# Scan loads by direction, two and three half steps ahead, and weights, sums and gates loaded through GpSimd's queue, in a one-core conformer, state-space and expert block

## The chip, the cores and the metric

The kernel runs on one core of one Trainium2 chip. The metric is the device time of one execution in microseconds; lower is better. The kernel before took 3031.84 us (median of three runs, 3028.96 to 3038.07).

## What is computed

A block of 1040 tokens (16 of them prepended) by 1024 features goes through an input projection of 9280 columns, which feeds a convolution branch (31 taps) and a two-way state-space scan in chunks of 128 tokens; both are gated, merged, added, and then a mixture of 16 experts follows. Cut to what matters here:

```python
proj = einsum('btd,dk->btk', rms_norm(h), w_in)           # conv, z, xbc, dt, gates
c = conf_a * sigmoid(conf_g); c = depthwise_conv(c, w_conf_dw, b_conf_dw)
xbc = silu(depthwise_conv(xbc, w_ssm_conv, b_ssm_conv))   # 7 taps -> xs, B, C
# per direction, chunk of 128 and group of 8 heads (32 heads, 4 groups):
decay  = exp(where(mask, a_cs[l] - a_cs[s], -inf))
y_diag = einsum(C, B, decay, xd);  state = state * exp(a_cs[-1]) + B^T (decay_to_end * xd)
y_off  = einsum(C, state_before, exp(a_cs))
y = rms_norm((y_forward + y_backward + d_skip * xs) * silu(z))
h = h + (gate0 * (silu(layer_norm(c)) @ w_conf_out) + gate1 * (y @ w_ssm_out)) @ w_out
out = rms_norm(h + expert_choice_ffn(rms_norm(h)))
```

## The kernel before

The program is one function, `tile_block`. Its stages follow one another: the input is normalized and transposed (to some 45 us); the 73 column tiles of the input projection run, and from about 137 us on the state-space scan runs between them (to 1227 us); then the two output projections and the merge (to some 1750 us); then the experts. The change touches the second stage alone.

**The projection.** `Columns` holds the order of the 73 weight tiles (128 columns each, 1024 by 128 values of 4 bytes). `group` loads three tiles at a time (L194), squares them on ScalarE (L196), sums the squares over partitions with a small matmul (L202) and makes scales (L206 to L212). `convert` splits a tile in a high and a low half-precision part, the first on ScalarE (L223), the second on VectorE (L224). `take` is called once per tile: at every third tile it calls `group` for the next three, and it converts one tile ahead. Six buffers hold loaded tiles (`wraw` and `wraw2`, three each). A tile is then multiplied in three chunks of some 346 tokens, 24 matmuls of 128x346 each (`proj`, L97 to L99), into three PSUM buffers named `mm`.

**What a tile is for.** `do_conf` takes two tiles for one block of the convolution, writes the gated input `ci` (L326), and puts 30 taps (L334, one VectorE instruction over 1040 tokens each) and the store of the result into the list `taps`; `some_taps(n)` takes n from it. `ci` has one buffer, and `do_conf` begins by emptying the list. `xbc_tile` writes `pre` (L374), makes six taps (L380), a silu (L381) and stores; its transposes (`turn`, L395 and L399) come eight thirds of a tile later. `z_tile` and `gate_tile` write `st` (L345, L355 to L357) and store it; the pool `stage` has four buffers.

**The scan.** For each of 4 groups and 9 chunks there is one unit of work within the chunk (`within`, `add_within`) and two half steps of the running state, one forward and one backward (`state`, `pass_state`): 36 units, 72 half steps. `within` loads B and C (`bc_`, L578), for both directions the running sums of the decay, repeated on all partitions (`row`, 512 KB each, L581), and the inputs `xk` (L538); ScalarE turns each `row` to decays (L599 eight times, L600), VectorE multiplies (L545, L602), and 32 matmuls of a unit add into `py` (L614). A half step loads `xk`, `Cc` (L629) and `er` (L633), multiplies the state (L646) and updates it (L652, L658, L660). `sum_of` loads the skip term `xa` (L555, ten buffers); `add_to` adds each part, and with the last one loads silu(z) into a buffer of `er` (L567), multiplies (L568) and stores `yz_d` (L569).

**What sets the order.** All loads of this stage are issued by SyncE's queue (SP), all stores by GpSimd's (POOL); a queue works in order, and an instruction that waits for a buffer holds what stands behind it. `plan` says which projection tiles lie beside each group of the scan. `fill` moves the projection on between half steps. Each instruction's place on its engine comes from a planner, which takes what is ready by its order in the program; `tc.high_priority(offset=n)` moves an instruction up by n places in that order.

The loop over half steps reads, with `prepare` as the three parts of `within`:

```python
for n, (g, d, c) in enumerate(halves):
    m = n % per
    if n % 2 == 0 and n // 2 + 1 < len(units):
        terms.append(prepare(units[n // 2 + 1]))
    with ahead():
        if n + 2 < len(halves):
            ops.append(state(*halves[n + 2]))
    if n % 2 == 0:
        add_within(*units[n // 2], terms.pop(0))
    fill(g, (m + 0.5) / per)
    S[d] = pass_state(g, d, c, S[d], ops.pop(0))
    fill(g, (m + 1) / per)
```

Of the kernel before, what the change touches and what calls it, by code (L numbers as in the profile page):

```python
# [18 lines left out]
P = 128  # L19
# [3 lines left out]
KD = 8  # L23
# [22 lines left out]
def tile_block(ctx, tc, x, meta_tokens, w_norm_mix, w_in, w_conf_dw, b_conf_dw, conf_ln_g, conf_ln_b,  # L46
# [117 lines left out]
    with tpool("upool", side="right") as upool, tpool("stage", bufs=4, side="right") as stage, \  # L164
# [11 lines left out]
        class Columns:  # L176
# [7 lines left out]
            def group(self, behind=None):  # L184
                b = self.G * self.groups
                cols = self.order[b:b + self.G]
                self.groups += 1
                n = len(cols)
# [3 lines left out]
                for i, col in enumerate(cols):  # L192
                    t = (wraw if (b + i) % 6 < 3 else wraw2).tile([P, KD, P], F32, name="wr")
                    nc.sync.dma_start(t, w_in[0][:, col:col + P].rearrange("(k p) c -> p k c", p=P))  # L194
                    with tc.high_priority(offset=400):
                        act.activation(out=junk, in_=t, func=AF.Square, accum_out=sq[:, i:i + 1])  # L196
                    self.raw[b + i] = t
                sqb = wsm.tile([P, 4], BF, name="sqb")
                dve.tensor_copy(sqb[:, :n], sq[:, :n])
# [27 lines left out]
            def take(self, col):  # L227
# [4 lines left out]
                if n == 0:  # L232
                    self.group(turned)
                    self.convert(0)
                if n % self.G == 0:
                    self.group(None if n else turned)
# [75 lines left out]
        def do_conf(j):  # L312
            wa, wg = wtile(j * P), wtile(D + j * P)
            some_taps(TK)
            ci = cfp.tile([P, T + 30], F32, name="ci")
            pool.memset(ci[:, 0:15], 0.0)
            pool.memset(ci[:, T + 15:T + 30], 0.0)
            for t0, n in NCH:
# [8 lines left out]
                yield  # L327
            co = cfp.tile([P, T], F32, name="co")
# [162 lines left out]
        def c_(j):  # L491
# [6 lines left out]
                z_(14, 15) + c_(5) + g_(9, 10) + c_(6) + g_(11, 12) + c_(7) + g_(13, 14, 15)]  # L498
# [18 lines left out]
        with tpool("b1") as b1:  # L517
# [12 lines left out]
            with tpool("s2", bufs=2) as s2, tpool("sps", bufs=1, space=PSUM) as sps:  # L530
# [4 lines left out]
                def load_xk(g, c):  # L535
                    L = TOK[c][1]
                    xk = s2.tile([P, 640], F32, name="xk", bufs=3)
                    nc.sync.dma_start(xk[:L], xk_d[g][c, :L])  # L538
                    return xk

                def scaled(g, xk, c, w, d):
# [3 lines left out]
                    dve.tensor_mul(heads(o[:L]), heads(xk[:L, :512]),  # L545
# [13 lines left out]
                def add_to(g, c, y):  # L559
                    t0, L = TOK[c]  # L560
                    s = sums[g, c]
                    dve.tensor_add(s[0][:, :, :L], s[0][:, :, :L], y[:, :, :L])
# [824 lines left out]
```

## Time and profile before

| | |
|---|---|
| runs, us | 3028.96, 3031.84, 3038.07 |
| profiled execution, us | 3033.02, span 3031.3 |
| mean granted TensorE clock | 0.956 of full speed |
| TensorE matmul (PE) busy | 2757.7 us, 91% |
| VectorE (DVE) busy | 2245.9 us, 74% |
| ScalarE (ACT) busy | 1714.3 us, 57% |
| GpSimd (POOL) busy | 501.3 us, 17% |

The profile is of one execution. A view by stretches gives the busy time of each engine in a part of the span; a table of waits tells which engine stood idle, before which line, and what released it; a timeline shows single instructions with the idle time ahead of them. L97 is line 97 of the kernel before.

### The profile page before, as it was taken

The page shows a single profiled execution, that of the slowest core. Times are in us where ns is not written, and L with a number is a line of the kernel's source. Part 1 is how long each engine was busy: PE and PEld are TensorE (multiplying, and loading weights), DVE is VectorE, ACT ScalarE, POOL GpSimd, SP SyncE. Part 2 cuts the span into 40 slices and gives each one's busy share as a digit, 9 for nine tenths or more (in the row PEclk, how much of TensorE's full clock was granted, in tenths as well). Part 3 has the DMA queues.
Part 4 walks back from the last instruction along what each step waited for, and adds up shares of the span by engine and source line. Part 5 has one row for each costly group of instructions (what it writes and reads, how often), then busy time and mean ns, then how long its engine had stood idle before and what let it go on. Part 6 is the DMA issues. An engine that isn't in the chain of part 4 may idle for free. (4 is left out here: it accounts for less than half of the span.)

```text
span 3031.3 us, 65413 instructions
## 1 busy us (share of the span) xinstructions
PE 2757.7 (91%) x27584; PEld 2364.2 (78%) x27584; DVE 2245.9 (74%) x3023; ACT 1714.3 (57%) x2551; POOL 501.3 (17%) x546
## 2 busy tenths in 40 slices
PE   6989989978988977889999789999999999999995
PEld 4656656655655655788978789999999999999995
DVE  6958886988996898797555678677777677777763
ACT  6657656556665531444213466666666666666643
POOL 1120021011012001341000002122221122222213
PEclk9999989989999988999999899999999999999997
DMA  5356667556658552522533889999999999999994
GB/s 145 105 157 197 182 179 212 159 163 202 190 160 242 173 163 77 174 75 74 164 116 115 294 298 335 330 333 328 329 333 333 327 337 332 331 335 335 334 322 139
DMA packets 424374, 691.89 MB, mean 228 GB/s; under 512 B 41313, under 2 KB 197825, under 8 KB 424073
## 3 DMA queue, kind: packets, MB, share of 16 engines
q1 hardware_dynamic: 386832, 584.61, 57.8%
q0 software_dynamic: 27168, 71.70, 8.1%
q10 hardware_dynamic: 10080, 31.40, 3.3%
q8 instruction: 216, 3.54, 0.5%
q14 instruction: 78, 0.64, 0.1%
HBM read 612.61 MB, written 75.01 MB: 227 GB/s over the span
## 5 line engine op out<-in xcount | busy, mean ns | idle before, releaser
L97 PE MATMUL gu<-xT,wh 128*128 128x130 f16 x3968 | 697.0, 222 | 2.3 <-ACT sil L1160 1.8
L99 PE MATMUL gu<-xT,wl 128*128 128x130 f16 x3968 | 696.0, 220 | 1.1 <-DVE wl L1131 1.1
L98 PE MATMUL gu<-xT,wh 128*128 128x130 f16 x3968 | 696.8, 219 | 0.0
L1117 ACT ACTIVATE junk<-wst 128x2048 bf16<-128x2048 f32 x248 | 473.8, 1910 | 382.6 <-DMA wst<-in_w_exp_gate_dram 317.5
L1131 DVE SCALAR_TENSOR_TENSOR wl<-wst,sc,wh 128x2048 f16<-128x2048 f32 x248 | 572.4, 2345 | 21.0 <-ACT wh L1128 17.6
L98 PEld LDWEIGHTS <-wh 128*128 128x128 f16 x4856 | 480.9, 99 | 91.7 <-issue 45.9
L97 PEld LDWEIGHTS <-wh 128*128 128x128 f16 x4856 | 475.6, 98 | 57.6 <-issue 12.5
L99 PEld LDWEIGHTS <-wl 128*128 128x128 f16 x4832 | 469.3, 97 | 45.6 <-DVE wl L1131 1.5
L1183 PE MATMUL dn<-ac,wst 128*128 128x130 f32 x3840 | 459.3, 277 | 0.0
L1183 PEld LDWEIGHTS dn<-ac,wst 128*128 128x128 f32 x3840 | 440.7, 191 | 0.0
L1202 POOL DMA_INDIRECT h<-yo,idx x60 | 186.6, 3110 | 901.9 <-DVE yo L1201 746.1
L334 DVE SCALAR_TENSOR_TENSOR co<-ci,ct,co 128x1040 f32<-128x1040 f32 x240 | 314.9, 1312 | 2.8 <-ACT co L331 0.3
L97 PE MATMUL mm<-uh,wh 128*128 128x346 f16 (+3 forms) x888 | 283.4, 319 | 31.5 <-DVE ci L326 17.3
L97 PE MATMUL mm<-uh,wl 128*128 128x346 f16 (+1 forms) x864 | 271.6, 314 | 18.2 <-ACT pre L374 9.6
L98 PE MATMUL mm<-ul,wh 128*128 128x346 f16 (+3 forms) x888 | 283.1, 319 | 0.0
L99 PE MATMUL mm<-uh,wh 128*128 128x346 f16 (+3 forms) x888 | 282.0, 318 | 0.0
L98 PE MATMUL mm<-ul,wl 128*128 128x346 f16 (+1 forms) x864 | 271.2, 314 | 0.0
L99 PE MATMUL mm<-uh,wl 128*128 128x346 f16 (+1 forms) x864 | 270.9, 314 | 0.0
L1128 ACT ACTIVATE wh<-wst,sc 128x2048 f16<-128x2048 f32 x124 | 241.3, 1996 | 17.3 <-DVE sc L1094 16.6
L599 ACT ACTIVATE row<-row,cst 128x128 f32<-128x128 f32 (+1 forms) x576 | 169.7, 378 | 116.9 <-DMA row<-cs_d 112.7
L380 DVE SCALAR_TENSOR_TENSOR po<-pre,sp,po 128x1040 f32<-128x1040 f32 x144 | 185.5, 1293 | 6.0 <-ACT po L377 5.7
L97 PE MATMUL mm<-yh,wh 128*128 128x346 f32 (+1 forms) x480 | 158.9, 338 | 25.1 <-DVE acc L802 14.9
(428 smaller groups left out, 4722.3 us busy)
## 6 DMA issues: line engine op xcount, KB each, us to landing
wst<-in_w_exp_gate_dram SPq DMA_DIRECT2D x128, 1024.0 KB, 8.2
wst<-in_w_exp_up_dram SPq DMA_DIRECT2D x128, 1024.0 KB, 8.0
wst<-in_w_exp_down_dram SPq DMA_DIRECT2D x128, 1024.0 KB, 9.8
wr<-in_w_in_dram SPq DMA_DIRECT2D x73, 512.0 KB, 4.7
row<-cs_d SPq DMA_DIRECT2D x64, 512.0 KB, 5.6
xk<-xk_d SPq DMA_DIRECT2D x92, 320.0 KB, 3.5
er<-ecs_d SPq DMA_DIRECT2D x120, 128.0 KB, 3.4
xk_d<-xt POOLq DMA_DIRECT2D x40, 256.0 KB, 3.3
```

What stands on the lines that cost most here:

```text
L97: pe.matmul(ps, wh(k), xh(k), start=(k == 0), stop=False)
L98: pe.matmul(ps, wh(k), xl(k), start=False, stop=False)
L99: pe.matmul(ps, wl(k), xh(k), start=False, stop=(k == K - 1))
L334: dve.scalar_tensor_tensor(co, ci[:, m:m + T], ct[:, m:m + 1], co, op0=OP.mult, op1=OP.add)
L380: dve.scalar_tensor_tensor(po, pre[:, m:m + T], sp[:, j, m:m + 1], po, op0=OP.mult, op1=OP.add)
L599: act.activation(out=E[:L, j, :L], in_=E[:L, j, :L], func=AF.Relu, scale=-1.0, bias=cs)
L1117: act.activation(out=junk, in_=t[m][b], func=AF.Square, accum_out=sq[:, b, m:m + 1])
L1128: act.activation(out=wh[m][0], in_=t[m][0], func=AF.Copy, scale=sc[:, 1, m:m + 1])
L1131: dve.scalar_tensor_tensor(wl[m][b], t[m][b], sc[:, 1, m:m + 1], wh[m][b], op0=OP.mult, op1=OP.subtract)
L1183: pe.matmul(last["dn"][b // 3][:, b % 3], t[:, k, b * P:b * P + P], ac[:, 2 * i + k], start=(i + k == 0 and b % 3 == 0), stop=(i == 7 and ...
L1202: nc.gpsimd.indirect_dma_start(out=h2_d[b], in_=yo[:, h], in_offset=None, compute_op=OP.add, out_offset=bass.IndirectOffsetOnAxis(ap=r.idx ...
```

## The change

Five edits, all in the projection and scan stage:

- `group` is split in `load` and `scale`. `load` still comes at every third tile; `scale` (squares, sums, scales) comes one tile later and its squares lose their high priority. All weight loads but the first three go through GpSimd's queue.
- `within` works on one direction at a time, so that there are 72 steps in place of 36 units, each beside one half step of the state. `row` and `Bk` come three, and the other scan loads two half steps ahead of their use (in the loop: the first part of a step's generators at n + 3, the second at n + 2, the computation at n + 1). The B part of `xk` (columns 512 to 639) becomes a load of its own, `Bk`; `xk` has four buffers of 512 columns instead of three of 640.
- `xa` (now nine buffers) and silu(z), now `sz` with one buffer, are loaded through GpSimd's queue. The product with silu(z) and the store of `yz_d` are put off by two thirds of a tile, and the product is written over `xa`; `er` serves the half steps alone.
- `ci` has two buffers, and `do_conf` empties the list of taps after the projection instead of before it.
- In the last group one gate tile moves from before to behind the second and third block of the convolution, six taps in place of five are taken per half step, and what is left of the transposes is done one half step earlier.

Cut to its core:

```diff
-            def group(self, behind=None):
+            def load(self):
                 b = self.G * self.groups
...
+                    (nc.gpsimd if b else nc.sync).dma_start(t, w_in[0][:, col:col + P].rearrange("(k p) c -> p k c", p=P))
+                    self.raw[b + i] = t
+
+            def scale(self, b, behind=None):
...
-                    with tc.high_priority(offset=400):
-                        act.activation(out=junk, in_=t, func=AF.Square, accum_out=sq[:, i:i + 1])
+                for i in range(n):
+                    act.activation(out=junk, in_=self.raw[b + i], func=AF.Square, accum_out=sq[:, i:i + 1])
...
                 if n % self.G == 0:
-                    self.group(None if n else turned)
+                    self.load()
+                if n % self.G == 1:
+                    self.scale(n - 1 + self.G)
...
-            some_taps(TK)
-            ci = cfp.tile([P, T + 30], F32, name="ci")
+            ci = cfp.tile([P, T + 30], F32, name="ci", bufs=2)
...
+            some_taps(TK)
             co = cfp.tile([P, T], F32, name="co")
...
-                z_(14, 15) + c_(5) + g_(9, 10) + c_(6) + g_(11, 12) + c_(7) + g_(13, 14, 15)]
+                z_(14, 15) + c_(5) + g_(9) + c_(6) + g_(10, 11) + c_(7) + g_(12, 13, 14, 15)]
...
-                        xa = s2.tile([P, 4, P], F32, name="xa", bufs=10)
-                        nc.sync.dma_start(xa[:, :, :L], xs_d[g][:, :, t0:t0 + L].rearrange("i p t -> p i t"))
+                        xa = s2.tile([P, 4, P], F32, name="xa", bufs=9)
+                        nc.gpsimd.dma_start(xa[:, :, :L], xs_d[g][:, :, t0:t0 + L].rearrange("i p t -> p i t"))
...
-                        sz = s2.tile([P, 4, P], F32, name="er")
-                        nc.sync.dma_start(sz[:, :, :L], sz_d[g][:, :, t0:t0 + L].rearrange("i p t -> p i t"))
...
+                        sz = s2.tile([P, 4, P], F32, name="sz", bufs=1)
+                        nc.gpsimd.dma_start(sz[:, :, :L], sz_d[g][:, :, t0:t0 + L].rearrange("i p t -> p i t"))
+                        finish.append((third[0] + 2, lambda: gated_out(g, c, xa, sz[:, :, :L])))
...
+                steps = [(within(*u), state(*h)) for u, h in zip(units, halves)]
...
+                for n in range(-3, len(steps)):
+                    with tc.high_priority(offset=600):
+                        for k in (3, 2):
+                            for s_ in steps[n + k] if 0 <= n + k < len(steps) else ():
+                                next(s_)
+                    if 0 <= n + 1 < len(steps):
+                        terms = [next(s_) for s_ in steps[n + 1]]
...
+                    (g, c, d), (xw, E) = units[n], ready[0]
                     m = n % per
...
+                    add_within(g, c, d, xw, E)
                     fill(g, (m + 0.5) / per)
...
+                    S[d] = pass_state(g, d, c, S[d], ready[1])
+                    ready = terms
                     fill(g, (m + 1) / per)
-                    if m == per - 3:
+                    if m == per - 4:
...
-                    some_taps((2, 4, 3, 5)[g])
+                    some_taps((2, 4, 3, 6)[g])
```

How this moves instructions shows at three places. In the rows below a name after L is the line of the kernel that the rows are of, so lines of the changed kernel are some ten to thirty higher. **SyncE's queue, between the first and the second group of the scan.** Before:

```order
L567 DMA er<-sz_d_67 128x4x128
L629 DMA Cc<-bc_d_61 128x16
L578 DMA bc__4894<-bc_d_62 128x2x128
L194 DMA wr<-in_w_in_dram 128x8x128 x2
L633 DMA er<-ecs_d 64x512 x2
L194 DMA wr<-in_w_in_dram 128x8x128
L567 DMA er<-sz_d_67 128x4x128
L581 DMA row<-cs_d 128x1024 x2
L629 DMA Cc<-bc_d_62 128x128
```

With the change (`Bk` is the B part of `xk`):

```order
L644 DMA Cc<-bc_d_61 128x16
L648 DMA er<-ecs_d 64x512 x2
L640 DMA Bk<-xk_d_76 128x128
L595 DMA bc__4650<-bc_d_62 128x2x128
L591 DMA row<-cs_d 128x8x16
L644 DMA Cc<-bc_d_62 128x128
L640 DMA Bk<-xk_d_76 128x128
L644 DMA Cc<-bc_d_62 128x128
L595 DMA bc__4924<-bc_d_62 128x2x128
L648 DMA er<-ecs_d 64x512 x2
```

The weight loads `wr` and the loads of silu(z) (`er<-sz_d`) are gone from this queue, and the `row` of one direction comes by itself, ahead of loads for later steps.

**GpSimd's queue, at the z tiles 14 and 15 in the last group.** Before there are stores alone:

```order
L358 DMA sz_d_70<-st 128x348
L358 DMA sz_d_70<-st 128x346
L569 DMA yz_d_73<-er 128x4x128
L358 DMA sz_d_70<-st 128x346
L569 DMA yz_d_73<-er 128x4x16
L358 DMA sz_d_70<-st 128x348
L358 DMA sz_d_70<-st 128x346 x2
L358 DMA sz_d_70<-st 128x348
L358 DMA sz_d_70<-st 128x346 x2
```

With the change weight loads and a load of silu(z) stand between the stores:

```order
L363 DMA sz_d_70<-st 128x348
L363 DMA sz_d_70<-st 128x346 x2
L189 DMA wr<-in_w_in_dram 128x8x128 x2
L363 DMA sz_d_70<-st 128x348
L363 DMA sz_d_70<-st 128x346 x2
L189 DMA wr<-in_w_in_dram 128x8x128
L363 DMA sz_d_70<-st 128x348
L363 DMA sz_d_70<-st 128x346
L573 DMA sz<-sz_d_70 128x4x128
L363 DMA sz_d_70<-st 128x346
L189 DMA wr<-in_w_in_dram 128x8x128 x3
```

Behind the trains of two, one and three weight loads stand the stores of `st`, which before stood behind one another.

**VectorE, at the last block of the convolution** (`co` is a tap, `ci` its input; `er`, `xa`, `S`, `xw` belong to the scan). Before:

```order
L334 SCALAR_TENSOR_TENSOR co<-ci,ct,co 128x1040 x2
L568 TENSOR_TENSOR er<-er,xa 128x512 x2
L334 SCALAR_TENSOR_TENSOR co<-ci,ct,co 128x1040 x3
L568 TENSOR_TENSOR er<-er,xa 128x4x16
L326 SCALAR_TENSOR_TENSOR ci<-sg,mm 128x348
L326 SCALAR_TENSOR_TENSOR ci<-sg,mm 128x346 x2
L224 SCALAR_TENSOR_TENSOR wh<-wr,sc,wh 128x8x128
L334 SCALAR_TENSOR_TENSOR co<-ci,ct,co 128x1040 x7
```

With the change (here the last of the three writes of `ci` alone):

```order
L614 TENSOR_TENSOR row<-row,cbm_11553 128x1024
L339 SCALAR_TENSOR_TENSOR co<-ci,ct,co 128x1040
L580 TENSOR_TENSOR xa<-xa,sz 128x512
L330 SCALAR_TENSOR_TENSOR ci<-sg,mm 128x346
L226 SCALAR_TENSOR_TENSOR wl<-wr,sc,wl 128x8x128
L339 SCALAR_TENSOR_TENSOR co<-ci,ct,co 128x1040
L667 TENSOR_TENSOR er<-yo,er 128x512
L679 TENSOR_TENSOR S_11657<-st,S_11657 128x512
L550 TENSOR_TENSOR xw<-xk,dtw 128x512
L339 SCALAR_TENSOR_TENSOR co<-ci,ct,co 128x1040
L568 TENSOR_TENSOR xa<-xa,er 128x512
```

Before, all taps of the block ahead (`co`) precede the writes of `ci`, and 30 taps are left behind the last write; with the change the write stands among them, with 54 taps behind it. Behind the first `yl` (VectorE's part of the output projection that comes next) there were 5 taps and are 27.

## Rows read from the trace of the kernel before

**Rows 1.** Engines by stretch: us, each engine's busy time (x instructions), clock, DMA, GB/s.

```profile
137.00:300.00 163.00, 146.95 (x1033) 97.85 (x1032) 113.44 (x155) 110.68 (x213) 23.25 (x51) 0.96 0.58 175
300.00:560.00 260.00, 237.43 (x1719) 161.55 (x1718) 210.83 (x300) 161.11 (x325) 32.65 (x63) 0.95 0.65 190
560.00:830.00 270.00, 234.52 (x1648) 158.17 (x1646) 242.64 (x327) 162.01 (x317) 31.37 (x66) 0.92 0.61 180
830.00:1060.00 230.00, 208.64 (x1514) 142.51 (x1514) 182.68 (x263) 141.87 (x285) 32.78 (x59) 0.95 0.66 191
1060.00:1227.00 167.00, 126.74 (x852) 85.39 (x849) 150.88 (x180) 40.90 (x85) 17.35 (x31) 0.89 0.40 120
1227.00:1300.00 73.00, 65.17 (x370) 62.99 (x368) 53.49 (x38) 40.05 (x59) 28.69 (x11) 0.91 0.52 170
```

**Rows 2.** Waits of TensorE, 137 to 1227 us: total us, times, longest.

```profile
PE mm L395 <- ACT po L381: 26.1, 6, 7.5
PE mm L97 <- DVE ci L326: 17.3, 2, 16.4
PE mm L97 <- ACT xt L399: 15.9, 7, 6.1
PE cb L587 <- DVE cbm L592: 14.3, 5, 5.8
PE mm L97 <- ACT pre L374: 11.1, 5, 5.9
...
PE mm L395 <- ACT st L356: 8.5, 2, 5.1
```

**Rows 3.** Waits of ScalarE, the same stretch.

```profile
ACT row L599 <- DMA row<-cs_d: 112.7, 32, 10.2
ACT junk L196 <- DMA wr<-in_w_in_dram: 90.1, 32, 7.2
...
ACT pre L374 <- DMA xs_d<-pre: 21.6, 6, 9.2
```

**Rows 4.** Timeline of SyncE's queue at one such place: start us, us.

```profile
428.81 0.37 SPq L567 DMA_DIRECT2D er<-sz_d  x1
429.28 0.99 SPq L581 DMA_DIRECT2D row<-cs_d  x2
```

**Rows 5.** Timeline of ScalarE, then; idle time ahead in brackets.

```profile
433.57 1.28 ACT L599 ACTIVATE row<-row,cst 128x128 f32<-128x128 f32 x4 [5.04 <-DMA row<-cs_d]
434.76 1.05 ACT L381 ACTIVATE po<-po 128x1040 f32<-128x1040 f32 x1
```

**Rows 6.** Timeline of TensorE, then, and two matmuls of a projection without waits.

```profile
239.74 0.31 PE L99 MATMUL mm<-uh,wh 128*128 128x346 f16 x1
239.88 0.31 PE L97 MATMUL mm<-uh,wh 128*128 128x346 f16 x1
...
435.87 1.02 PE L395 MATMUL mm<-ident,po 128*16 128x128 f32 x4 [5.45 <-ACT po L381]
```

**Rows 7.** Waits of SyncE's queue, 137 to 1227 us.

```profile
SPq L633 <- DMA yz_d<-er: 73.1, 15, 13.1
...
SPq L581 <- PE py L614: 42.1, 20, 6.9
```

**Rows 8.** Waits of VectorE, 137 to 1227 us.

```profile
DVE er L568 <- DMA er<-sz_d: 27.7, 19, 4.6
```

**Rows 9.** Timeline of TensorE at its longest wait.

```profile
1183.36 0.45 PE L97 MATMUL mm<-uh,wh 128*128 128x346 f16 x1 [16.39 <-DVE ci L326]
```

**Rows 10.** Groups of instructions, VectorE: count | busy us, mean ns | idle before.

```profile
L334 DVE SCALAR_TENSOR_TENSOR co<-ci,ct,co 128x1040 f32<-128x1040 f32 x240 | 314.9, 1312 | 2.8 <-ACT co L331 0.3
```

**Rows 11.** DMA issues by line: count, KB each, median us from issue to landing.

```profile
wr<-in_w_in_dram SPq DMA_DIRECT2D x73, 512.0 KB, 4.7
sz_d<-st POOLq DMA_DIRECT2D x32, 173.0 KB, 4.4
```

**Rows 12.** Timeline of GpSimd: one store as its queue issues it.

```profile
424.42 0.76 POOL L569 DMA_DIRECT2D yz_d<-er  x1
```

More of the change, by code (lines that the diff above doesn't have):

```diff
@@ L232, in take @@
                 if n == 0:
-                    self.group(turned)
+                    self.load()
+                    self.scale(0, turned)
                     self.convert(0)
                 if n % self.G == 0:
-                    self.group(None if n else turned)
+                    self.load()
+                if n % self.G == 1:
+                    self.scale(n - 1 + self.G)
                 self.convert(n + 1)
@@ new lines, in tile_block, with within @@
+                shared = {}
+                def within(g, c, d):
+                    t0, L = TOK[c]
+                    h0 = HG * g + 32 * d
+                    assert all((g, i) in turned_ for i in range(5))
+                    E = s2.tile([P, HG, P], F32, name="row", bufs=4)
+                    nc.sync.dma_start(E[:, :, :L], cs_d[c, h0:h0 + HG, :L].partition_broadcast(P))
+                    yield
+                    if d == 0:
+                        bc_ = s2.tile([P, 2, P], F32, name="bc_")
+                        nc.sync.dma_start(bc_[:, :, :L], bc_d[g][:, :, t0:t0 + L])
+                        shared[g, c] = load_xk(g, c), []
+                        sum_of(g, c)
+                    xk, cbm = shared[g, c]
+                    yield
+                    if d == 0:
+                        ps = sps.tile([P, P], F32, name="cb")
+                        pe.matmul(ps[:L, :L], bc_[:, 0, :L], bc_[:, 1, :L], start=True, stop=True)
+                        with ahead():
+                            for b in range(2):
+                                cbm.append(s2.tile([P, P], F32, name=f"cbm{b}"))
+                                dve.tensor_mul(cbm[b][:L, :L], ps[:L, :L], tri["ge" if b else "le"][:L, :L])
+                    with ahead():
@@ L634, in state @@
                                               ecs_d[c, hh, q:q + 4, :L].partition_broadcast(64))
-                    return xk, xw, er, Cc
+                    yield
+                    if xk is not None:
+                        with ahead():
+                            xw = scaled(g, xk, c, 1, d)
+                    yield Bk, xw, er, Cc
                 def pass_state(g, d, c, S, ops):
                     t0, L = TOK[c]
-                    xk, xw, er, Cc = ops
+                    Bk, xw, er, Cc = ops
                     hs = slice(32 * d + HG * g, 32 * d + HG * g + HG)
@@ L661, in pass_state @@
                     return Sn
-                units = [(g, c) for g in range(GR) for c in range(NTT)]
+                units = [(g, c, d) for g in range(GR) for c in range(NTT) for d in range(2)]
                 halves = [(g, d, 8 - i if d else i) for g in range(GR) for i in range(NTT) for d in range(2)]
@@ L676, in fill @@
                         done[0] += 1
-                def prepare(unit):
-                    w_ = within(*unit)
-                    with ahead():
-                        next(w_)
-                    next(w_)
-                    with ahead():
-                        return next(w_)
-                terms = [prepare(units[0])]
-                with ahead():
-                    ops = [state(*halves[0]), state(*halves[1])]
-                per = len(halves) // GR
-                for n, (g, d, c) in enumerate(halves):
-                    m = n % per
-                    if n % 2 == 0 and n // 2 + 1 < len(units):
-                        terms.append(prepare(units[n // 2 + 1]))
-                    with ahead():
-                        if n + 2 < len(halves):
-                            ops.append(state(*halves[n + 2]))
-                    if n % 2 == 0:
-                        add_within(*units[n // 2], terms.pop(0))
+                        if finish and finish[0][0] <= third[0]:
+                            finish.pop(0)[1]()
@@ L706, in tile_block @@
                 for _ in work:
                     pass
+                while finish:
+                    finish.pop(0)[1]()
                 some_taps(TK)
```

92 lines of the change are left out of this document (39 added, 53 removed).

## The prediction

> **What bounds the kernel now.** The page comes first: TensorE is busy 91% of the span, no other engine over 74%, so what is to be won is TensorE's idle time and its slow clock in the one stage that the change touches. The view by stretches then shows that stage, 137 to 1227 us [rows 1]. In its five stretches TensorE is busy 147.0, 237.4, 234.5, 208.6 and 126.7 us, 954.3 of 1090, so it idles 135.7. The granted clock of the five is 0.96, 0.95, 0.92, 0.95 and 0.89. One minus each, by its length, makes 6.5 + 13 + 21.6 + 11.5 + 18.4 = 71 us of full clock that were not granted; half or more of that lies under the idle time itself, where it costs nothing, so I count 36 us as lost to work at 1.2 in place of 2.4 GHz. More than 172 us cannot be won. VectorE is nearly as full: 243 of 270 us in the third stretch and 151 of 167 in the fifth, which leaves 27 and 16 us.
>
> Next, who keeps TensorE waiting [rows 2]. One wait of 16.4 us is for the convolution's input `ci`. ScalarE's results end waits of 26.1 (silu), 15.9 (transposes copied out), 11.1 and 8.5 us (projection chunks copied out), 61.6 in all; VectorE's masks `cbm` end 14.3. ScalarE is only half busy, so the question is what it waits for [rows 3]: 112.7 us in 32 waits for `row`, 90.1 us in 32 waits for a weight tile that it is to square. One case shows the chain. SyncE issues two `row` loads at 429.28, right behind a load of silu(z) in the same queue [rows 4]; ScalarE has stood 5.04 us for them at 433.57, and the silu of another tile stands behind the first four of them [rows 5]; the transposes that need that silu start at 435.87 after 5.45 us of idle TensorE [rows 6]. So work that needs no scan load is held up by one that came late. SyncE's queue itself is held by buffers: 73.1 us for stores of `yz_d` that must leave the `er` buffers, 42.1 us for `py` to give up a `row` buffer [rows 7].
>
> **The change part by part.**
>
> *Second `ci`, taps behind the projection.* Before, the last block of the convolution can't write `ci` until the 30 taps ahead are done; its wait and a small one make 17.3 us [rows 2], 16.39 of them in one piece [rows 9]. With two buffers both go: 17 us.
>
> *Loads ahead, squares behind.* The 1090 us hold 72 half steps, 15 us each, and the `row` loads of the case above let ScalarE begin 4.3 us after their issue [rows 4, 5]. Issued three half steps ahead instead of in the step that uses it, it is there; so is a weight tile squared one tile (72 matmuls, at 0.14 us [rows 6] some 10 us) after its load, which lands in 4.7 us [rows 11]. Scales are still needed two tiles later, which covers the small chain behind the squares, so the later squares cost nothing. Of the 61.6 us a part is not ScalarE's waiting for loads: it also stood 21.6 us for stores of `pre` [rows 3], which stay. 202.8 of 224.4 us is nine tenths, 56 us; as `row` has four buffers still and its load waits for `py` as before [rows 7], I take three quarters of it, 42 us, with 20 and 61.6 as ends. Of the 14.3 us for `cbm` I take 10 (0 to 14.3), as VectorE no longer stands for silu(z), which it did for 27.7 us [rows 8].
>
> *Clock.* Idle removed is 17 + 42 + 10 = 69 of 135.7 us; the same share of 36 us is 18. Gross: 87 us, with 118 (93 + 25) as the upper end.
>
> *VectorE.* The third and fifth stretch hold 75.7 of the 135.7 us, so 49 of the 87 should come there, and VectorE has 43 us of room. But the order on VectorE puts 27 taps behind the first `yl` of the next stage, where there were 5. 22 taps of 1.31 us [rows 10] are 29 us less in the fifth stretch, and 29 us more behind 1227, where VectorE has 73.0 - 53.5 = 19.5 us free until 1300 [rows 1]. The 9 us over are a loss to the output projection.
>
> *GpSimd's queue.* It takes over 70 weight loads, 36 of `xa` and 36 of silu(z). At the 0.76 us of a 256 KB store's issue [rows 12] that is 108 us more on an engine that is busy 137 of 1090 us [rows 1]: no bound. What counts is order: a store behind one to three weight loads of 4.7 us each [rows 11] lands later than 4.4 us, and ScalarE then waits for a `st` buffer. No row shows such a store. At least it costs nothing, since two chunks of a tile (24 matmuls each, 3.4 us) may pass before `st` is needed again; at most 62 us (second rival). Most trains are short, so I take 20.
>
> Would VectorE hold up these issues? The store above was issued in 0.76 us [rows 12] in a stretch where VectorE is busy 211 of 260 us [rows 1]; I let it count for the 142. A rule of the Trainium skill stands against this step (SBUF — State Buffer, section "SBUF: two separate sides"): a DMA of GpSimd's queue can't get its descriptors written while VectorE runs an operation that takes the port pair the two share. By the row the sum is as here; by the rule it would be that of the fourth rival.
>
> *At no cost:* 64 `Bk` loads of 64 KB on a queue that loses 142 others, hidden behind two half steps; without that cover they would cost ScalarE nothing and TensorE one landing each. One `sz` buffer: at most one chunk is finished per half step of 15 us, against the landing of a load of half a weight tile's size and one product. The first loads of the program: SyncE has three weight tiles fewer between the inputs, a gain of a few us at best. Plan and rate of taps: the same work in another order. The earlier transposes at a group's end come when their tiles are a half step younger; late then would be the silu, as before.
>
> **Sum.** 87 - 9 - 20 = 58 us. The profiled execution took 3033.0 us, 1.2 over the median of the runs; 3033 - 58 = 2975 us.
>
> **The rivals.**
>
> *VectorE becomes the bound.* For it: 243 of 270 and 151 of 167 us busy [rows 1]. Against: half its remaining idle time there is itself waiting for ScalarE and loads, and taps spill. If only a third of the 43 us can be used, 15 us in place of 49 come from these two stretches: 87 - 34 - 9 - 20 = 24 us, 3009 us.
>
> *Stores behind weights (slower).* The place is GpSimd's queue at z and gate tiles. A store behind a train of three lands after 4.4 + 3 x 4.7 = 18.5 us. `st` covers two chunks and the `mm` buffers two more, 13.6 us together, so TensorE stands 4.9 us per train. It decides from the point where a store takes over 13.6 us. There are 23 trains; 32 of 73 tiles are of this kind, so 10 trains, 49 us, and with the slow clock behind them (36 / 135.7 more) 62. ScalarE then stands for stores as it stood for loads, so the 42 us and their clock, 53, don't come. 87 - 9 - 53 - 62 = -37: 3070 us. For it: in the order at the z tiles 14 and 15, trains of two, one and three stand between stores. Against: only a full train reaches that point.
>
> *The queue was not what held the loads.* SyncE's waits are for buffers, `py` among them [rows 7], and those waits go on. Then only `ci` counts: 17 and 5 of clock, less 9 and some 10 of stores, 3 us: 3030 us. Against: the `yz_d` waits in the same rows go, as `er` is no longer used for that. The Trainium skill says (DMA: Bandwidth & Descriptors, section "Issuing engines are not separate DMA queues") that loads from several engines run on the same DMA engines, and that issuing from more of them only saves issue time; by that rule this rival would be the likeliest. The rows on SyncE's waits speak against it: what a queue of its own saves here is waiting, not issuing.
>
> *GpSimd's issues held up.* Each moved issue lasts until the VectorE instruction then under way ends, say a tap: 0.76 + 1.31 = 2.1 us [rows 10, 12]. A train of three is out in 6.2 in place of 2.3 us, and 10 such trains make stores 4 us later, with the clock 50 us: 58 - 50 = 8 us, 3025 us. Against: the 0.76 us itself. It is the mechanism of the Trainium skill's page SBUF — State Buffer, named above.
>
> **How the numbers follow.** A measurement of this kernel can tell 0.3%, 9 us, from no change. Forecast 0.64 (gains of 30 to 100 us), VectorE 0.14, stores 0.13, queue not at fault 0.07, issues held up 0.02. Faster: the forecast and VectorE's case, 0.78; same: the last two but for a hundredth, 0.08; slower: that hundredth and the stores, 0.14. The range reaches from 2935 us (gross near its upper end, stores at nothing) to 3025 us, which takes in the VectorE case; outside lie the stores' case, half of the queue's and a little below, 0.2 in all.
>
> **What would show it.** In the profile with the change: ScalarE's waits for `row` and for weights fall from 203 us to under 60; TensorE's wait for `ci` is gone; its idle time between the start of the scan and the end of the projection falls from 136 to some 70 us, and the granted clock of these stretches is over 0.95. VectorE would be over 90% busy from the second group on, and taps run on into the output projection. The forecast is wrong if ScalarE's waits for stores (`st`, `pre`) or GpSimd's landing times grow by what the load waits lose, or if `row` loads still land just as ScalarE comes to them.

## Result and profile after

The changed kernel took 2987.47 us (median of four runs, 2985.32 to 2996.0) beside 3034.95 for the kernel before: a ratio of 0.9851, 95% interval 0.9824 to 0.9878, or 45 us less. The forecast was 2975 us in a range of 2935 to 3025. The time lies in the range, but several of the sum's terms were far off, in opposite directions, and the sections below are mostly about that.

The profiled execution took 2988.87 us (span 2987.1). The projection ended at 1170.9 us in place of 1221.7, the first expert matmul began at 1649.6 in place of 1695.9. So 51 us were won in the stage that the change touches, and 4.5 were given back up to the experts. The page's engine line, against 91, 74, 57 and 17% before:

```profile
PE 2750.6 (92%) x27584; PEld 2359.5 (79%) x27584; DVE 2240.1 (75%) x3023; ACT 1713.3 (57%) x2549; POOL 616.6 (21%) x688
```

Where in that stage? The view by stretches, cut near the first sum into `ci` of block 5 (1006 us before, 999 after): the kernel before, then the changed one (columns as in rows 1).

```profile
137.00:1000.00 863.00, 767.54 (x5460) 518.85 (x5459) 699.62 (x970) 543.03 (x1070) 116.27 (x232) 0.94 0.63 186
1000.00:1227.00 227.00, 186.74 (x1297) 126.62 (x1295) 200.86 (x252) 73.54 (x154) 21.12 (x38) 0.92 0.45 133
```

```profile
137.00:1000.00 863.00, 772.55 (x5501) 521.84 (x5499) 708.00 (x988) 549.49 (x1073) 213.92 (x352) 0.95 0.62 185
1000.00:1176.00 176.00, 170.95 (x1265) 116.31 (x1262) 162.05 (x217) 70.98 (x150) 29.45 (x47) 0.99 0.51 156
1176.00:1250.00 74.00, 60.27 (x328) 58.30 (x329) 72.05 (x49) 34.73 (x52) 26.63 (x9) 0.88 0.37 113
```

Up to 1000 us the changed kernel is 41 matmuls ahead, 6 us at 0.14 us each. All the rest, some 45 us, comes in the last stretch, where TensorE's idle time falls from 40 to 5 us and the granted clock rises from 0.92 to 0.99. VectorE is 92% busy there and 97% in the 74 us behind, where it makes the last block's taps.

TensorE's waits in the whole stage after (137 to 1176 us), which answer to [rows 2], and ScalarE's, which answer to [rows 3] (us, times, longest):

```profile
PE mm L400 <- ACT po L386: 35.4, 7, 10.4
PE mm L97 <- ACT xt L404: 15.0, 10, 4.6
PE cb L602 <- DVE cbm L606: 10.0, 7, 2.4
PE mm L97 <- ACT pre L379: 8.4, 5, 2.9
PE mm L400 <- ACT pre L379: 6.3, 5, 3.1
PE st L671 <- DVE S L679: 3.6, 1, 3.6
PE py L626 <- DVE row L614: 2.9, 1, 2.9
...
PE mm L400 <- ACT st L361: 1.6, 2, 1.0
...
PE mm L97 <- DVE ci L330: 0.3, 1, 0.3
```

```profile
ACT row L611 <- DMA row<-cs_d: 123.9, 44, 8.3
ACT junk L198 <- DMA wr<-in_w_in_dram: 70.8, 27, 7.5
...
ACT pre L379 <- DMA xs_d<-pre: 12.7, 3, 6.3
ACT st L361 <- DMA sz_d<-st: 6.6, 4, 3.3
```

The wait for `ci` is gone, as foretold. But silu, copied transposes and copied chunks hold TensorE for 35.4 + 15.0 + 8.4 + 1.6 = 60.4 us, where the same four rows made 61.6 (the 6.3 us, not counted in the sum, were 7.4); and ScalarE still waits 194.7 us for `row` and weights, where it waited 202.8. What the loads ahead were to win is not there. SyncE's two longest waits show that the loads of `row` (L591) still go out only as `py` gives up a buffer (before, that wait was 42.1 us in 20 [rows 7]):

```profile
SPq L591 <- PE py L626: 138.6, 50, 11.2
SPq L543 <- DVE xw L550: 134.4, 53, 6.0
```

### The profile page after: what moved, and what is told of

It reads as the page before. It is cut to its first block, busy times and chain, and to the rows that moved or that the text cites. A ratio compares the mean times of both kernels' runs of the same rounds, so it can differ in the third digit from the quotient of the medians.

```text
span 2987.1 us, 65478 instructions
## 1 busy us (share of the span) xinstructions
PE 2750.6 (92%) x27584; PEld 2359.5 (79%) x27584; DVE 2240.1 (75%) x3023; ACT 1713.3 (57%) x2549; POOL 616.6 (21%) x688
## 5 line engine op out<-in xcount | busy, mean ns | idle before, releaser
L339 DVE SCALAR_TENSOR_TENSOR co<-ci,ct,co 128x1040 f32<-128x1040 f32 x240 | 323.8, 1349 | 5.5 <-ACT co L336 3.8
L97 PE MATMUL mm<-uh,wh 128*128 128x346 f16 (+3 forms) x888 | 279.4, 315 | 17.4 <-ACT xt L404 8.1
L99 PE MATMUL mm<-uh,wh 128*128 128x346 f16 (+3 forms) x888 | 278.1, 314 | 0.0
L611 ACT ACTIVATE row<-row,cst 128x128 f32<-128x128 f32 (+1 forms) x576 | 170.8, 378 | 143.4 <-DMA row<-cs_d 123.9
```

What stands on the lines that cost most here:

```text
L97: pe.matmul(ps, wh(k), xh(k), start=(k == 0), stop=False)
L99: pe.matmul(ps, wl(k), xh(k), start=False, stop=(k == K - 1))
L339: dve.scalar_tensor_tensor(co, ci[:, m:m + T], ct[:, m:m + 1], co, op0=OP.mult, op1=OP.add)
L611: act.activation(out=E[:L, j, :L], in_=E[:L, j, :L], func=AF.Relu, scale=-1.0, bias=cs)
```

## Experiments

Two theories stood against each other. *First, the second `ci`*: it is worth far more than its own wait, and the loads, the queue and the squares little. *Second, the sum as put*: `ci` some 13 us net, the loads the rest. Each ratio below is to the kernel before on the same chip, with its 95% interval; the last column is the start of the first expert matmul in the profiled execution, behind which all kernels have the same instructions.

| kernel | ratio | interval | first expert, us |
|---|---|---|---|
| before | 1 | | 1695.9 |
| the change | 0.9851 | 0.9824 to 0.9878 | 1649.6 |
| e1 change, one `ci` | 1.0024 | 1.0009 to 1.004 | 1697.0 |
| e2 before, two `ci` | 0.9903 | 0.9884 to 0.9921 | 1658.7 |
| e3 weights on SyncE | 0.9879 | 0.986 to 0.9899 | 1659.9 |
| e4 squares with loads | 0.9905 | 0.9884 to 0.9926 | 1664.6 |
| e5 two `ci`, taps first | 0.9863 | 0.9841 to 0.9886 | 1652.9 |
| e6 three `row` | 0.9908 | 0.989 to 0.9927 | 1662.0 |
| e7 five `row` | 0.9884 | 0.9863 to 0.9906 | 1659.0 |
| e8 x tiles earlier | 0.9848 | 0.9829 to 0.9866 | 1645.9 |
| e9 e2 with the new plan | 0.9906 | 0.988 to 0.9933 | 1664.0 |
| e10 block 5 first | 0.9899 | 0.9872 to 0.9926 | 1659.0 |
| e11 block 5 a group earlier | 0.9869 | 0.9838 to 0.99 | 1650.2 |
| e12 ten taps | 0.9692 | 0.9676 to 0.9708 | 1597.2 |

### One `ci` taken from the change, two given to the kernel before

```diff
 wa, wg = wtile(j * P), wtile(D + j * P)
+some_taps(TK)
-ci = cfp.tile([P, T + 30], F32, name="ci", bufs=2)
+ci = cfp.tile([P, T + 30], F32, name="ci")
...
-some_taps(TK)
 co = cfp.tile([P, T], F32, name="co")
```

The second kernel is the kernel before with the same lines edited the other way.

> The changed kernel with one `ci` buffer and the taps ahead of the projection, as before; all else as changed. If the `ci` term of the sum is right, TensorE waits about 17 us for `ci` again (16 in one piece at the last block), the clock loses some 5, and 9 come back because about 5 taps, not 27, are left behind the projection's end: +13 us, some 3000 us. Rival: VectorE is so full in the last group that the taps only change place, and what the second buffer wins in the scan the output projection gives back: within 4 us of 2987.

> The kernel before with this part of the change alone: two `ci` buffers, the taps behind the block's projection. If the terms add, the wait of 17 us for `ci` goes with some 5 us of slow clock, less the 9 us that the later taps cost: -13 us, some 3022 us. Rival (taps only change place): within 4 us of 3035. If it gives 25 us or more, this part is half of the whole gain.

With one `ci` the whole gain is gone: 0.0024 over the kernel before, 52 us behind the change. With two, the kernel before gains 29 us, 37 by the first expert matmul. The sum had 13. Both expectations put it too low, the rivals lower still; only the last clause of the second, half of the gain or more, came true.

TensorE's waits behind 1000 us in e1 show where it goes. The same list of the changed kernel is empty up to the end of its projection. (Left out are 5.3 us for `yh`, which belong to the output projection, and 0.8 for `cbm`.)

```profile
PE st L671 <- DVE S L679: 14.3, 4, 4.3
PE mm L97 <- DVE ci L331: 11.6, 2, 8.5
PE yo L665 <- DVE S L679: 5.4, 3, 2.4
...
PE py L626 <- ACT row L611: 3.5, 1, 3.5
```

Only 11.6 us carry the name of `ci`; 23.2 us are for states and decays of the scan. The cause is the same, as the projection's matmuls (tile `mm`) on TensorE between 1023 and 1100 us show, in the change, in e1 and in the kernel before:

```profile
1023.00:1100.00 77.00, 59.48 (x393) 1.00 0.57 171
```

```profile
1023.00:1100.00 77.00, 25.98 (x172) 0.87 0.61 183
```

```profile
1023.00:1100.00 77.00, 40.30 (x268) 0.96 0.62 173
```

With two buffers 393 matmuls of the projection lie beside the scan in these 77 us, with one 172 or 268: block 6's first sum into `ci` waits for VectorE to end the 30 taps of block 5, so it comes at 1122.4 us in e1 against 1043.9 in the change. TensorE has only the scan's chain to work on meanwhile (state, product, state), and that chain waits for VectorE, which is full of taps; the clock falls to 0.87 as well. The kernel before shows the same waits in its last group, beside the 17.3 us for `ci` [rows 2]:

```profile
PE st L652 <- DVE S L660: 6.3, 6, 2.0
PE py L614 <- DVE xw L545: 5.4, 2, 3.7
PE py L614 <- DVE row L602: 5.4, 1, 5.4
```

### The buffer or the order of the taps

```diff
 wa, wg = wtile(j * P), wtile(D + j * P)
+some_taps(TK)
 ci = cfp.tile([P, T + 30], F32, name="ci", bufs=2)
...
-some_taps(TK)
 co = cfp.tile([P, T], F32, name="co")
```

> The changed kernel with two `ci` buffers, but the outstanding taps handed out ahead of the block's projection, as before. One `ci` cost 52 us, not the 13 of the sum. Theory A, the buffer: with one, the projection of blocks 6 and 7 can't be done until VectorE is through the taps, and TensorE has then only the scan's chain to work on; with two it may go ahead wherever the taps stand, so the time stays within 5 us of 2987. Theory B, the order: 30 taps in front of all else on VectorE delay sums, states and `ci` itself whatever the number of buffers; the time is near that with one, 3030 to 3045 us. In between, VectorE is late with `ci` behind the taps: a wait for `ci` of 5 to 10 us at blocks 6 and 7 and some 3000 us.

0.9863: the buffer alone does it (theory A). The place of the taps in the program moved the time by no more than the measurement is uncertain.

### The weights' queue and the squares, each undone

```diff
-(nc.gpsimd if b else nc.sync).dma_start(t, w_in[0][:, col:col + P]...)
+nc.sync.dma_start(t, w_in[0][:, col:col + P]...)
```

> The changed kernel with the weight tiles issued by SyncE again, the sums and silu(z) still by GpSimd. If the loads' own queue is what the change needed, weight tiles stand behind `row` loads that wait for `py`; ScalarE's waits for weights rise from 71 us to over 120 and the time by 15 to 35 us (3002 to 3022 us). Rival, that the queue was not what held the loads: within 5 us of 2987. Third: the stores on GpSimd's queue get freer and this wins: under 2980 us.

```diff
 if n % self.G == 0:
     self.load()
-if n % self.G == 1:
-    self.scale(n - 1 + self.G)
+    self.scale(n + self.G)
```

(and the squares at `tc.high_priority(offset=400)` again)

> The changed kernel with the squares in the same step as the loads and at high priority, as before. If squaring one tile later is a part of the gain, ScalarE's waits for weights rise from 71 us to about 110 and the time by 8 to 15 us (2995 to 3002 us). Rival: these waits lie in time that ScalarE has to spare (busy 620 of 1040 us), so the time stays within 4 us of 2987.

E3 is 0.0028 over the change, 8.5 us, with the intervals overlapping; e4 0.0054, 16 us. E4's loss is about what was expected of it, e3's lies between its theory and its rival. In neither do ScalarE's waits for weights rise as they should have, 76.4 us in e3 and 83.1 in e4 where over 120 and about 110 were expected, so what either costs can't be read from these waits.

For e3 the Trainium skill's rule (DMA: Bandwidth & Descriptors, section "Issuing engines are not separate DMA queues") is that spreading loads over issuing engines saves no more than the issue time. By it e3 would equal the change, and this run doesn't contradict it.

### Three and five `row` buffers

```diff
-E = s2.tile([P, HG, P], F32, name="row", bufs=4)
+E = s2.tile([P, HG, P], F32, name="row", bufs=3)
```

> The changed kernel with three `row` buffers instead of four. Theory: the buffers, not the place in the program or in a queue, set when a `row` load can go, which is why ScalarE still waits 124 us for `row`; then with three the waits at least double (over 250 us) and the time grows by 20 to 50 us (3007 to 3037 us). Rival: the load has slack and the waits are only ScalarE being early; within 6 us of 2987.

```diff
-E = s2.tile([P, HG, P], F32, name="row", bufs=4)
+E = s2.tile([P, HG, P], F32, name="row", bufs=5)
...
-Sn = s2.tile([P, 512], F32, name=f"S{d}")
+Sn = s2.tile([P, 512], F32, name=f"S{d}", bufs=1) if S is None else S
```

> The changed kernel with five `row` buffers; the room comes from the states, which are updated in place (one buffer for each direction instead of two). Theory that the buffers hold the loads and the waits for them cost: ScalarE's waits for `row` fall from 124 to under 40 us, TensorE's for silu and transposes copied out from 50 to some 30, and the time by 10 to 25 us (2962 to 2977 us). Rival, that ScalarE only waits there instead of elsewhere: the waits fall, the time stays within 4 us of 2987. If the states in place cost something, TensorE's waits for `S` grow from 3.6 us.

ScalarE's wait for `row` with three, then with five:

```profile
ACT row L611 <- DMA row<-cs_d: 130.9, 46, 9.1
```

```profile
ACT row L611 <- DMA row<-cs_d: 122.4, 42, 7.9
```

130.9, 123.9 and 122.4 us with three, four and five: the wait doesn't depend on the number of buffers, so the theory that the buffers explain it falls. Three cost 17 us all the same, less than that theory had and more than its rival, and five with the states in place cost 10 (TensorE's wait for `S` is 5.6 us, not enough to explain it). A likely reading, not tried, is that the planner puts the first operation on a `row` where it takes the load to have landed, so that with earlier loads ScalarE only reaches its wait earlier.

### The plan: x tiles, block 5, and the new plan alone

```diff
-c_(1) + x_(1, 1) + g_(2) + x_(1, 2, 3) + g_(3, 4)
+c_(1) + x_(1, 1, 2, 3) + g_(2, 3, 4)
...
-x_(2, 5, 0, 1) + g_(5) + x_(2, 2, 3) + c_(3)
+x_(2, 5, 0, 1, 2, 3) + g_(5) + c_(3)
...
-x_(3, 0, 1) + g_(6) + x_(3, 2, 3) + g_(7, 8)
+x_(3, 0, 1, 2, 3) + g_(6, 7, 8)
```

> The changed kernel with one gate tile in each of the first three groups' plans moved behind the last of the group's x tiles. TensorE waits longest where a group's last transposes are all drawn ahead, four half steps before its end (4.5 us at 414, 6.7 at 677, 10.4 at 930): with the x tiles three chunks earlier their silu is done by then. Theory, that these waits are real: -10 to -20 us (2967 to 2977 us) and TensorE's waits for `po` from 35 to some 15 us. Rival: three x tiles in a row make VectorE late and the waits come back elsewhere; within 4 us of 2987, or over.

TensorE's waits in e8, 137 to 1180 us:

```profile
PE mm L400 <- ACT pre L379: 22.6, 4, 8.9
PE mm L97 <- ACT st L350: 10.7, 4, 4.9
PE mm L97 <- ACT pre L379: 10.0, 6, 4.5
PE mm L204 <- ACT pre L379: 8.5, 2, 4.9
```

The 35.4 us for `po` are gone and the time is the same: these four rows make 51.8 us, where they made 15.9 in the changed kernel. They grew by as much as went. A wait removed at its name was not a wait removed.

```diff
-z_(14, 15) + c_(5) + g_(9) + c_(6) + g_(10, 11) + c_(7) + g_(12, 13, 14, 15)
+c_(5) + z_(14, 15) + c_(6) + g_(9, 10, 11) + c_(7) + g_(12, 13, 14, 15)
```

> The changed kernel with block 5 as the first item of the last group's plan, and block 6 right behind z 14 and 15. VectorE has no taps from 947 to 1021 us in the changed kernel (block 4 is done, block 5 not begun) and is 98% busy from 1060 to 1172. Theory: VectorE's taps at the end are what is left of the loss; begun some 40 us earlier, about 20 of them leave the time behind the projection's end, and waits there (19 us in all) fall by half: -8 to -15 us, ratio 0.980 to 0.982. Rival: TensorE is full in the last group whatever VectorE does, and silu and states are disturbed earlier; within 4 us of 2987 (0.984 to 0.9865).

```diff
-g_(7, 8) + z_(12, 13)
+z_(12, 13) + c_(5)
...
-z_(14, 15) + c_(5) + g_(9) + c_(6) + g_(10, 11) + c_(7) + g_(12, 13, 14, 15)
+z_(14, 15) + g_(7) + c_(6) + g_(8, 9, 10) + c_(7) + g_(11, 12, 13, 14, 15)
```

> The same further: block 5 in place of the two gate tiles in the third group's plan, behind z 12 and 13; the gate tiles fill the last group. By the theory of the run before, -10 to -20 us (ratio 0.978 to 0.982), and the output projection waits under 8 us from its start on. Rival: the third group's VectorE, which carries the x tiles' convolutions, gets later by block 5's sums and nothing is won: 0.984 to 0.988.

Neither wins, and e10, 15 us over the change, is slower than its rival had it. In e10 block 5's taps begin at 997.7 in place of 1021.2 us, but block 7's end at 1245.6 in place of 1246.9. In e11 the taps do go: block 7's thirty are done at 1199.3 us.

```profile
L339 DVE SCALAR_TENSOR_TENSOR co<-ci,ct,co x30: 1286/1297/3464, 1139.3 to 1198.0; 128x1040 f32<-128x1040 f32 x30
```

Its projection ends at 1166.5 us, 4 before the changed kernel's, and yet the first expert matmul comes at 1650.2 against 1649.6. So ending the taps 48 us sooner won nothing: the theory of both runs, that these taps are what is left of the loss, falls.

The kernel before with two `ci` and the new plan of the last group, 6 taps a half step:

```diff
-z_(14, 15) + c_(5) + g_(9, 10) + c_(6) + g_(11, 12) + c_(7) + g_(13, 14, 15)
+z_(14, 15) + c_(5) + g_(9) + c_(6) + g_(10, 11) + c_(7) + g_(12, 13, 14, 15)
...
-some_taps((2, 4, 3, 5)[g])
+some_taps((2, 4, 3, 6)[g])
```

> The kernel before with two `ci` buffers, the taps behind the projection, and the last group's plan and rate of taps as changed (gate 9 alone, then 10 and 11; 6 taps a half step); no load, queue or square is changed. With two `ci` alone its projection ended at 1167.8 us, 3 us before the changed kernel's, and the output projection then waited 18.8 us, because block 7 could not start in `co` until the taps of block 6 were stored. Theory: what the loads ahead, GpSimd's queue and the late squares seemed to add (16 us between the ratios 0.9903 and 0.9851) is this wait and the noise of two measurements; then this kernel comes within 7 us of the changed one (ratio 0.983 to 0.988). Rival: the loads are worth their 16 us; then it stays at 0.990 and its waits for `cbm`, `pre` and `po` outside the last group are longer than the changed kernel's by that much.

0.9906, as without the plan: the rival holds, and the loads, the queue and the squares together bring some 16 us by the ratios (9 by the first expert matmul of e2, 14 by that of e9). Where does it lie? Up to 1000 us e2 is as far as the change, 5509 matmuls against 5501:

```profile
137.00:1000.00 863.00, 768.87 (x5509) 521.03 (x5507) 705.90 (x984) 547.84 (x1080) 116.73 (x233) 0.95 0.62 187
```

So the loads win nothing up to there. E2 loses behind the projection, where TensorE waits for the output projection's first input, and ScalarE, which makes that input, stands for a store:

```profile
PE mm L97 <- ACT yh L776: 18.8, 1, 18.8
```

```profile
ACT co L331 <- DMA conf_d<-co: 15.3, 1, 15.3
```

Block 7 can't start in the single buffer `co` until block 6's taps are made and stored. They end at 1180.8 us in e2 and 1187.1 in e9, but 1170.4 in the change, where TensorE waits 6.4 us. Which part of the change makes block 6's taps end earlier was not taken apart.

### Most taps left out

```diff
-taps.extend([lambda m=m: tap(m) for m in range(1, TK)])
+taps.extend([lambda m=m: tap(m) for m in range(1, 11)])
```

> The changed kernel with 10 of the 30 VectorE taps of each convolution block; 20 are left out, so the convolution is cut short. This takes 20 x 8 x 1.35 = 216 us off VectorE, 189 of them in the seven blocks behind 137 us. TensorE's idle time of some 90 us between the scan's start and the end of the projection stayed at 85 to 95 us in every kernel with two `ci`, however the loads, buffers and tiles were placed. Theory, VectorE's fullness sets it: the idle time falls under 50 us, the projection ends before 1130 us, and the time falls by over 40 us (under 2945 us). Rival, the chains through ScalarE (silu, copies of transposes, its order) set it: the idle time stays over 75 us, the projection ends at 1155 to 1170, and only the waits behind it (19 us) go: -10 to -20 us (2967 to 2977 us).

2941 us, 48 below the change by the ratios; the projection ends at 1129.1 us. The stretch up to 1140 us, TensorE's longest waits, and ScalarE's longest:

```profile
137.00:1140.00 1003.00, 936.36 (x6769) 632.30 (x6767) 727.37 (x1078) 614.32 (x1209) 241.44 (x394) 0.97 0.64 192
```

```profile
PE mm L97 <- ACT xt L404: 19.1, 5, 9.3
PE mm L97 <- ACT yh L796: 11.0, 2, 7.9
```

```profile
ACT row L611 <- DMA row<-cs_d: 146.4, 46, 8.9
```

Up to the end of the projection TensorE idles 66.6 - 7.9 = 59 us (the 7.9 are the wait for `yh`, behind it) where it idled 90: not under 50 as the theory had it, but far from the rival's 75. Time and end of the projection are the theory's. So with the taps about a third of that idle time goes. The wait for silu, 35.4 us, no longer appears, though its line on ScalarE is untouched; and ScalarE waits *longer* for `row`, 146.4 in place of 123.9 us. So the length of ScalarE's waits for loads doesn't tell what TensorE loses by them.

How fewer taps take the silu's wait away is less plain. The silu needs six of VectorE's taps first, but the planner also orders ScalarE anew when VectorE's work changes. The seven waits for silu of the changed kernel can be followed back one by one. In none did a load come last: where ScalarE had just stood 8.0 us for a `row` (until 602.5 us) and 5.9 (until 905.2), the last tap ended later still, at 602.8 and 906.3. In the longest, VectorE did not come last either (TensorE, then VectorE's last tap, then ScalarE):

```profile
930.47 2.09 PE L400 MATMUL mm<-ident,po 128*16 128x128 f32 x9 [10.40 <-ACT po L386]
917.76 1.28 DVE L385 SCALAR_TENSOR_TENSOR po<-pre,sp,po 128x1040 f32<-128x1040 f32 x1
919.53 2.45 ACT L611 ACTIVATE row<-row,cst 128x128 f32<-128x128 f32 x8 [4.31 <-DVE cbm L606]
924.53 2.46 ACT L611 ACTIVATE row<-row,cst 128x128 f32<-128x128 f32 x8 [0.19 <-DMA row<-cs_d]
926.90 1.04 ACT L198 ACTIVATE junk<-wr 128x1024 bf16<-128x1024 f32 x1
929.35 1.07 ACT L386 ACTIVATE po<-po 128x1040 f32<-128x1040 f32 x1
```

The last tap is done at 919.04 us, and ScalarE works on two `row` and makes a square ahead of the silu, which starts 10.3 us later. At 676.87 us (6.66 us of idle TensorE) two `row` stand ahead of the silu again. With ten taps the same last silu starts 1.9 us behind its last tap. So the ten taps changed two things, VectorE's load and ScalarE's order, and this run doesn't part them.

## Why the prediction held, and where it was wrong

| step of the sum | put at | found |
|---|---|---|
| second `ci`, its wait (13 with 5 of clock, less 9) | 17 | the wait 17.3, then 0.3; the edit 29 alone (e2), 52 when taken away (e1) |
| loads ahead, squares behind | 42 | the same four rows: 61.6, then 60.4: 1 |
| `cbm` | 10 | 14.3, then 10.0: 4 |
| idle time of the stage, these three | 69 | 135.7, then 95.5: 40 |
| clock | 18 | TensorE busy 954.3, then 943.5: 11 |
| taps behind the projection | -9 | 4.5 given back in all, not by the taps (e11) |
| stores behind weights | -20 | nothing seen |
| net | 58 | 45 by the ratio, 46 at the first expert |

*The step "second `ci`" failed by its size.* It counted the wait that carries the buffer's name. The buffer did more: it let the projection of blocks 6 and 7 run beside the scan, and with that the waits for states, `xw` and decays behind 1000 us went (17 us in the rows above) and the clock of that stretch rose to 0.99. In the whole stage these three waits made 21.0 us before and 6.5 after; the prediction put them at nothing without a reason, 10.2 us for `S` among them, more than the 8.5 that it counted for a chunk copied out. The values don't add either: 29 us alone, 52 on top of the rest, and the rest without it is 7 us slower than nothing.

*The step "loads ahead, squares behind" failed.* "202.8 of 224.4 us is nine tenths" took ScalarE's waits as the cause of TensorE's. Most of them are ScalarE being early. They hardly moved with the change (194.7), the ones for `row` not with three or five buffers, and those grew when TensorE idled less (e12). The line set beforehand, "under 60", is missed by far, and so is idle time at "some 70". The evidence that I had was one case, at 433 us, where the chain did run that way. It was not the rule: of the five waits for silu over 1 us in the kernel before, 25.8 us, this is the only one (5.45 us) in which a load came last, and of the seven in the changed kernel there is none.

*The step "VectorE" had the right place but not the right cost.* Taps do run into the output projection, and VectorE is full (92 and 97%) from 1000 to 1250 us; but from 300 to 567 it was at 85% and from 837 to 1060 at 78%, not over 90. The 9 us for the taps behind the projection are not borne out: with these taps done 48 us sooner (e11) the time from the projection's end to the experts was 484 us against 479. The rival "VectorE becomes the bound" has a part in what is left, at most the third of the idle time that went in e12; the order on ScalarE has another. Its time, 3009, was too late because the `ci` term was too small in it as well.

*The rival "stores behind weights" is refuted.* Weight tiles do land later on GpSimd's queue, 6.4 against 4.7 us, but gate stores land in 3.2 against 2.8 and silu(z) stores in 3.5 against 4.4 [rows 11], and ScalarE's waits for stores of `st` and `pre` fell from 21.6 + 5.5 = 27.1 us to 12.7 + 6.6 = 19.3. Taking the 20 us off was a second error, which hid part of the first.

*The rival "the queue was not what held the loads" was right in its mechanism.* SyncE's waits for buffers went on and grew (138.6 us for `py`). Its time, 3030, failed with the `ci` term. *"GpSimd's issues held up"* is refuted by the issue times, below.

So the total was near by luck: the 42 us of the loads' term, of which 1 came where it was put, were made up by a `ci` term over twice too small and by two costs that were not paid. What stays open is what makes the last 9 to 16 us: the loads by direction and ahead, the queue or the squares. Undoing the weights' queue or the squares alone (e3, e4) costs 8.5 and 16 us by the ratios, as much as all of them bring, and the projection then ends at 1182.8 and 1179.7 us, though with all of them undone (e2) it ends at 1167.8. So they don't add, and each edit also gives the planner another order on every engine. The change further moves the computations of a step up by 300 places instead of 600, which the list of edits doesn't name; that was not tried alone, and neither was the work by direction. No complete version tried beats the changed kernel; e8 equals it.

## What to carry to other kernels

A buffer is worth the work that it lets another engine do meanwhile, not the wait that carries its name: look at what TensorE has left to run while the buffer is held, and count the waits that appear because only a dependent chain is left. An off-path engine's waits are no evidence by themselves; before pricing them, follow several of the bottleneck's waits back past the engine named, or take work off the engine behind it, as with the ten taps, and then look whether the order of the other engines changed too. And judge a forecast by its terms: a right total from two wrong ones will not carry over.

## What was unexpected in the hardware

GpSimd's DMA issues were not slowed by a VectorE that was 82% busy (708 of 863 us up to 1000 us). All 70 weight loads of 512 KB were issued in 0.88 to 0.95 us each (count, min, median and max in ns, first and last start), though a tap lasts 1.30:

```profile
L189 POOL DMA_DIRECT2D wr<-in_w_in_dram x70: 882/897/952, 17.5 to 1044.3; - x70
```

A load of silu(z), 256 KB, took 0.76 us, as the store of that size did before [rows 12]; and the taps up to 1000 us lasted 1295 ns in the median, 1293 before. The Trainium skill's rule that GpSimd can't write its DMAs' descriptors while VectorE runs an operation in a two-port mode (SBUF — State Buffer, section "SBUF: two separate sides") doesn't show in this trace; whether VectorE ran an operation of that kind here isn't shown. Where GpSimd computes, it does matter: taps of block 7 beside GpSimd's sums of squares last up to 3.49 us in place of 1.30 (min, median, max of the taps from 1169 us on; then one tap and the sum beside it).

```profile
L339 DVE SCALAR_TENSOR_TENSOR co<-ci,ct,co x31: 1287/1302/3487, 1169.1 to 1245.6; 128x1040 f32<-128x1040 f32 x31
```

```profile
1183.82 3.45 DVE L339 SCALAR_TENSOR_TENSOR co<-ci,ct,co 128x1040 f32<-128x1040 f32 x1
1182.73 3.44 POOL L799 TENSOR_TENSOR ssq<-ssq,yst 128x1040 f32<-128x1040 f32 x1 [9.01 <-ACT yst L798]
```

The sum began first and ended at 1186.17 us, the tap 1.10 us behind it. That the same section makes the two engines' shared port pair an exclusive lock, held for a whole instruction, agrees with these rows.

Last, the expert stage, with the same instructions in all kernels, took 1318 to 1331 us from its first matmul to TensorE's last in the profiled executions, so differences under some 10 us between two of these can't be laid to the stage that was edited.
